# A two-layer decoder trunk on one core: queries and keys projected token-major, normed and then turned; scores of two query blocks together; inverse roots as a power on GpSimd

## The chip, the core and the metric

The kernel runs on one core of a Trainium2 chip. TensorE (PE) multiplies matrices into PSUM, VectorE (DVE), ScalarE (ACT) and GpSimd (POOL) work on SBUF tiles of 128 partitions, SyncE (SP) issues the loads. The metric is the device time of one execution in microseconds.

## What is computed

Two layers on x of 512 tokens by 1024 features, float32. Layer 0: RMS norm, one projection to 16 heads of 64 (8 forgetting heads and 8 stick-breaking heads, and 8 gate logits), causal attention, output projection, residual, then a gated MLP with a width-3 convolution. Layer 1: a gated short convolution in place of attention, and such an MLP. The change touches layer 0's attention and, in one helper, all four norms:

```python
xn = rms_norm(h, norm_g)
proj = xn @ w_in
q, k, v = heads(...), heads(...), heads(...)        # 16 heads of 64
q_fox, k_fox = rms_norm(q[:, :8], fox_q_g), rms_norm(k[:, :8], fox_k_g)
q_sb, k_sb = rms_norm(q[:, 8:], sb_q_g), rms_norm(k[:, 8:], sb_k_g)
# forgetting: softmax(q k / 8 + F_q - F_k) v;  F: running sum of log_sigmoid(gate)
# stick-breaking: sigmoid(z) times the product of sigmoid(-z) over later keys, times v
h = h + concat(o_fox, o_sb) @ w_out
```

## The kernel before

Activations stay on the chip with features on partitions: `hs_hi` and `hs_lo` are [128, 8, 512], feature block by token. Float32 products are three single-pass products of halves, x = hi + lo with hi rounded to float32r: hi hi, lo hi, hi lo. A weight chunk (512 KB) is loaded by SP (L220), its high half made by ACT (L223) and its low half by DVE (L226); three chunks are kept split, and `weights()` has `AHEAD` = 2 asked for in advance. The norm's scale by token is not applied to the input but to the products.

PSUM has eight banks under three names: two of `a` (projections, weighted sums, output), four of `b` (scores), two of `c` (transposes, small sums).

Queries and keys (`queries_keys`, L497) come by pairs of heads, p = 0 to 7, four forgetting pairs first. The weights stand in PE and 512 tokens stream by (L237 to L239, 24 products of 512 columns a bank), so the result has head features on partitions. ACT squares the bank (L552) and copies it out with the gain (L560, or L556 for a stick-breaking query). A norm over a head's 64 features is a sum over partitions: four matmuls of the squares with two columns of ones (L511, each a step of its own, `SUM_STEP` apart), then Newton's method for the inverse root in 12 DVE instructions (`rsqrt`, L299), a copy that spreads the result over 64 columns (L535), transposes to get it along the tokens (L542), a product (L544) and the split into halves (L320, L321). A stick-breaking query keeps its scale apart; the sigmoids take it as their scale (L600, L601).

Values (`values`, L459) are token-major: 128 tokens of `hs` stand in PE, 256 weight columns (four heads; 264 with the gates) stream by (L480 to L482), and ACT and DVE scale the bank by token on the way out (L473, L474).

`logits(p, b)` (L563) gives the scores of a pair's two heads for 128 queries: three products of 64 rows per head (L576), the decay (L580), the mask (L582), into two banks `b`; then softmax (L591 to L596) or the two sigmoids, a product scan and a product (L600 to L604). `turn` (L609) transposes the weights (L623) and splits them (L626, L627); `weigh` (L630) multiplies them by the values (L642, L643) and adds the two halves (L652, L653).

The program's order is written out by hand. `spend` counts PE microseconds emitted, `after` puts a step behind so many of them, `fill(us)` emits from `fillers`, a list of generators of independent products (projections of later pairs, values, the first half of the output projection). For block g the main loop (L750) emits the scores of block g, a fill of `FILL1`, every second time the weighted sum of block g - 2, the turning of block g - 1 and a fill of `FILL2`. `need` emits fillers until something is there. The framework's scheduler may move an instruction past others of its engine whose inputs it expects later. At the start, the first queries and keys run while x arrives and its norm is made; the norm's scale comes from `Norm.scale` (L267), its row form from `spread` (L274) after `NROWS`.

Of the kernel before, what the change touches and what calls it, by code (L numbers as in the profile page):

```python
# [20 lines left out]
I32 = mybir.dt.int32  # L21
# [17 lines left out]
WB = 4  # L39
PRE = 12.0  # L40
# [3 lines left out]
SUMS, ROWS = 3.0, 5.0  # L44
NSUMS, NROWS = 4.0, 3.0
FILL1, FILL2 = 1.0, 2.6
# [3 lines left out]
def trunk(  # L50
# [48 lines left out]
    # a row a column of `gains`: the norms after the first and the conv taps  # L99
# [27 lines left out]
    head_ones = const.tile([P, 2], F32, tag="head_ones", name="head_ones")  # L127
    pool.memset(head_ones, 0.0)
    pool.memset(head_ones[0:HD, 0:1], 1.0)
    pool.memset(head_ones[HD:P, 1:2], 1.0)  # L130
# [104 lines left out]
    def mm3(acc, w, rhs, first, last):  # L235
        """acc += w.T @ rhs of two pairs of halves."""
# [10 lines left out]
    class Norm:  # L247
        """Gathers the squares of a block's input and gives its RMS scale by token:
        `col` [token, block] on partitions and `row` along the free axis on all of them."""
# [17 lines left out]
        def scale(self, sums):  # L267
# [3 lines left out]
            rsqrt(self.col, v, NB, self.name)  # L271
# [11 lines left out]
        def scaled(self, fn):  # L283
            """Runs what needs `row` when it is there."""
# [14 lines left out]
    def rsqrt(dst, v, n, name):  # L299
        """dst = v ** -0.5 by Newton's method."""  # L300
        def t(tag, dt=F32):
            return tiny.tile([P, n], dt, tag=f"{tag}{n}", name=f"{tag}_{name}")
        half = t("rh")
        dve.tensor_scalar(half, v, -0.5, None, op0=ALU.mult)
        shifted = t("rs", I32)
        dve.tensor_scalar(shifted, v.bitcast(I32), 1, None, op0=ALU.logical_shift_right)
        guess = t("rg", I32)
        dve.tensor_scalar(guess, shifted, -1, 0x5F3759DF, op0=ALU.mult, op1=ALU.add)
        y = guess.bitcast(F32)
        for i in range(3):  # L310
            a = t("ra")
            dve.tensor_tensor(a, y, y, op=ALU.mult)
            b = t("rb")
            dve.tensor_tensor(b, a, half, op=ALU.mult)
            z = dst if i == 2 else t("ry")
            dve.scalar_tensor_tensor(z, b, 1.5, y, op0=ALU.add, op1=ALU.mult)
            y = z
# [5 lines left out]
    def causal_conv(dst, src, tap):  # L323
        """dst[t] = tap(2) src[t] + tap(1) src[t-1] + tap(0) src[t-2]."""
# [9 lines left out]
    def want_qk(p):  # L334
        want(w_in, 0, 8, D + p * P, P)
        want(w_in, 0, 8, p * P, P)

    def want_v(g):
        for k in range(0, 8, 4):
            want(w_in, k, 4, 2 * D + g * 256, 256, *((QKV, 8) if g == 0 else ()))  # L340
# [5 lines left out]
    want_qk(0)  # L346
    for g, ps_ in enumerate(((1, 2), (3, 4), (5, 6), (7,))):
        if g == 0:
            want_v(0)
        for p_ in ps_:  # L350
            want_qk(p_)
        if g < 3:
            want_v(g + 1)
# [39 lines left out]
    # ================= attention =================  # L393
# [4 lines left out]
    def choose():  # L398
        """Columns of 0 and 1 that pick the rows of `dl` and `dr`."""
# [25 lines left out]
    def log_gate():  # L425
        """The gates' log-sigmoid, its running sums on the partitions of `dl`."""
# [6 lines left out]
        wide = work.tile([P, S], F32, tag="u0", name="fwide").rearrange("p (b c) -> p b c", b=NB)  # L433
# [6 lines left out]
    def decay(wide):  # L440
# [9 lines left out]
        both = work.tile([P, S], F32, tag="u0", name="fboth")  # L450
# [8 lines left out]
    def values(g):  # L459
# [37 lines left out]
    def queries_keys(p):  # L497
# [12 lines left out]
        def sums(i, sq, b, t):  # L510
            pe.matmul(t[:, 2 * b:2 * b + 2], sq[:, b * P:(b + 1) * P], head_ones, start=True, stop=True)  # L511
            if b == NB - 1:
# [4 lines left out]
                if i == 1:  # L517
                    scales()
# [386 lines left out]
```

## Time and profile before

| | |
|---|---|
| three runs | 1233.95, 1235.51, 1236.94 us; median 1235.51 |
| the profiled execution | span 1231.8 us from the first to the last instruction; its time outside the span is not recorded |
| instructions | 14998, of them 5861 matmuls |
| engines, share of the span | PE 99%, weight loads 80%, DVE 62%, ACT 41%, POOL 2% |
| mean granted TensorE clock | 0.997 |
| loads | 108.13 MB, 88 GB/s over the span |

The profile is one execution seen by the hardware's profiler. A row of instructions gives start, duration, engine, line, operation, operands, shape; two or more of a kind in a row are merged (x4). A matmul's record runs on until its last result is modelled to be out, so the records of a stream overlap, and its true pace is the distance between starts. A group's row gives count, busy time and the mean of one in nanoseconds, then the engine's idle time before them and what ended it.

### The profile page before, as it was taken

How to read it: one execution, taken by the hardware profiler on the slowest of the kernel's cores; microseconds unless marked ns; L12 is line 12 of the kernel's file. 1: busy time of each engine (PE TensorE's matmuls, PEld its weight loads, DVE VectorE, ACT ScalarE, POOL GpSimd, SP SyncE). 2: the span in 40 equal slices, each digit the busy share in tenths (PEclk: the TensorE clock that was granted, in tenths of full speed). 3: DMA queues.
4: the chain of work that ended last, by engine and by line, in shares of the span. 5: the costliest groups of instructions: out<-in, count | busy, mean ns of one | idle time of the engine just before them, and what ended most of it. 6: DMA issues, size and time to landing. Idle time of an engine off the chain costs nothing.

```text
span 1231.8 us, 14998 instructions
## 1 busy us (share of the span) xinstructions
PE 1214.5 (99%) x5861; PEld 987.9 (80%) x5861; DVE 762.9 (62%) x1256; ACT 500.7 (41%) x779; POOL 21.5 (2%) x104
## 2 busy tenths in 40 slices
PE   8999999999999999999999999999999999999998
PEld 7887878767888888888888888888888888888886
DVE  5786878887776777673333555555767776762222
ACT  6455665655443434342222222233444434342120
POOL 3000000000000000000000000000000000000000
PEclk9999999999999999999999999999999999999999
DMA  6312121212333332323333333332333333322330
GB/s 177 104 36 69 36 69 36 69 52 69 95 93 100 89 102 86 103 79 95 94 94 101 91 97 99 89 101 87 91 98 92 96 95 93 98 91 86 118 105 35
DMA packets 183463, 108.13 MB, mean 88 GB/s; under 512 B 4604, under 2 KB 176684, under 8 KB 183392
## 3 DMA queue, kind: packets, MB, share of 16 engines
q1 hardware_dynamic: 183136, 107.01, 29.5%
q8 instruction: 46, 0.75, 0.3%
q0 software_dynamic: 256, 0.16, 0.1%
q14 instruction: 25, 0.20, 0.0%
HBM read 105.06 MB, written 2.10 MB: 87 GB/s over the span
## 4 chain that ended last, share of the span: by engine, by line
PE 94%; DVE 4%; ACT 1%; DMA 1%; issue 0%; SPq 0%; DVEq 0%; ACTq 0%
PE psa L237 13%; PE psa L239 13%; PE psa L238 13%; PE psb L237 11%; PE psb L239 11%; PE psb L238 11%; PE psa L480 3%; PE psa L482 3%; PE psa L481 3%; PE psb L481 2%; PE psb L480 2%; PE psb L482 2%; PE psb L576 1%; DVE rest L603 1%; PE psc L623 1%; PE psa L642 1%
## 5 line engine op out<-in xcount | busy, mean ns | idle before, releaser
L223 ACT ACTIVATE whi<-raw 128x1024 fp32r<-128x1024 f32 (+1 forms) x198 | 208.3, 1053 | 365.9 <-PE psb L238 127.0
L226 DVE TENSOR_TENSOR wlo<-raw,whi 128x1024 fp32r<-128x1024 f32 (+1 forms) x198 | 240.1, 1213 | 162.3 <-ACT whi L223 161.4
L237 PE MATMUL psa<-hs_hi,whi 128*128 128x512 f32 x544 | 220.4, 405 | 0.5 <-DVE o L653 0.5
L239 PE MATMUL psa<-hs_hi,wlo 128*128 128x512 f32 x544 | 215.5, 396 | 0.0
L238 PE MATMUL psa<-hs_lo,whi 128*128 128x512 f32 x544 | 215.0, 395 | 0.0
L237 PE MATMUL psb<-hs_hi,whi 128*128 128x512 f32 x480 | 189.9, 396 | 0.0
L239 PE MATMUL psb<-hs_hi,wlo 128*128 128x512 f32 x480 | 189.8, 395 | 0.0
L238 PE MATMUL psb<-hs_lo,whi 128*128 128x512 f32 x480 | 188.8, 393 | 0.0
L328 DVE SCALAR_TENSOR_TENSOR u<-y,taps,u 128x510 f32<-128x510 f32 (+1 forms) x176 | 131.0, 747 | 3.0
L239 PEld LDWEIGHTS psa<-hs_hi,wlo 128*128 128x128 f32 x544 | 102.2, 188 | 24.0
L237 PEld LDWEIGHTS psa<-hs_hi,whi 128*128 128x128 f32 x544 | 102.7, 189 | 21.8 <-PE psb L582 0.6
L238 PEld LDWEIGHTS psa<-hs_lo,whi 128*128 128x128 f32 x544 | 102.6, 189 | 21.4
L238 PEld LDWEIGHTS psb<-hs_lo,whi 128*128 128x128 f32 x480 | 90.1, 188 | 21.4
L239 PEld LDWEIGHTS psb<-hs_hi,wlo 128*128 128x128 f32 x480 | 90.1, 188 | 21.4
L237 PEld LDWEIGHTS psb<-hs_hi,whi 128*128 128x128 f32 x480 | 90.3, 188 | 20.3
L779 DVE TENSOR_TENSOR y<-psb,nrow_n 128x512 f32<-128x512 f32 x44 | 30.4, 691 | 83.9 <-PE psb L239 83.9
L320 ACT ACTIVATE a<-u 128x512 fp32r<-128x512 f32 x44 | 27.8, 633 | 118.7 <-DVE u L784 118.7
L783 ACT ACTIVATE u<-u 128x512 f32<-128x512 f32 x44 | 27.8, 632 | 91.4 <-DVE u L328 91.4
L325 ACT ACTIVATE u<-y,taps 128x512 f32<-128x512 f32 x88 | 62.9, 717 | 0.0
L321 DVE TENSOR_TENSOR a<-u,a 128x512 fp32r<-128x512 f32 x44 | 30.4, 692 | 29.4 <-ACT a L320 29.4
L480 PE MATMUL psa<-whi,hs_hi 128*128 128x256 f32 (+1 forms) x128 | 38.6, 303 | 0.0
L482 PE MATMUL psa<-whi,hs_lo 128*128 128x256 f32 (+1 forms) x128 | 36.2, 283 | 0.0
(226 smaller groups left out, 1851.0 us busy)
## 6 DMA issues: line engine op xcount, KB each, us to landing
raw<-in_ffn_w_up SPq DMA_DIRECT2D x88, 512.0 KB, 3.8
raw<-in_ffn_w_down SPq DMA_DIRECT2D x30, 512.0 KB, 3.7
raw<-in_attn_w_in SPq DMA_DIRECT2D x24, 512.0 KB, 3.9
raw<-in_conv_w_in SPq DMA_DIRECT2D x24, 512.0 KB, 3.8
raw<-in_ffn_w_down SPq DMA_DIRECT2D x16, 448.0 KB, 3.7
raw<-in_attn_w_out SPq DMA_DIRECT2D x8, 512.0 KB, 3.4
raw<-in_conv_w_out SPq DMA_DIRECT2D x8, 512.0 KB, 3.9
x_tok<-in_x SPq DMA_DIRECT2D x4, 512.0 KB, 7.9
```

The lines of the kernel that those rows point to most:

```text
L223: made = act.activation(hi[:, 0:nk * n], raw[:, 0:nk * n], AF.Copy)
L226: dve.tensor_tensor(lo[:, 0:nk * n], raw[:, 0:nk * n], f32(hi[:, 0:nk * n]), op=ALU.subtract)
L237: pe.matmul(acc, w[0], rhs[0], start=first, stop=False)
L238: pe.matmul(acc, w[0], rhs[1], start=False, stop=False)
L239: pe.matmul(acc, w[1], rhs[0], start=False, stop=last)
L321: dve.tensor_tensor(lo, src, f32(hi), op=ALU.subtract)
L325: act.activation(dst, src, AF.Copy, scale=tap(2))
L328: dve.scalar_tensor_tensor(dst[:, d:], src[:, 0:S - d], tap(j), dst[:, d:], op0=ALU.mult, op1=ALU.add)
L480: pe.matmul(acc, lhs[0], w[0], start=first, stop=False)
L481: pe.matmul(acc, lhs[0], w[1], start=False, stop=False)
L482: pe.matmul(acc, lhs[1], w[0], start=False, stop=last)
L779: dve.tensor_tensor(y, acc, norm.row, op=ALU.mult)
```

## The change

Queries and keys are projected like the values, in four groups of four heads (`columns`, `heads`), values of group 0 first. Each block of 128 tokens is then normed where a head's features lie along the free axis: ACT squares, DVE sums by head, POOL makes the scale in three steps, DVE multiplies from PSUM. `turn_heads(p)` transposes the normed block of a pair and splits it with the gain on the way out; both kinds of heads have their scale in the queries. `rsqrt` becomes one POOL instruction with a power, in the four norms as well. `logits` and `turn` take two query blocks at a time: four banks `b` at once, one tile of weights per head. A filler can be held back until its tiles are free, and the quotas are others (`PRE`, `FILL2`, a `FILL1` in `turn` after each block and one ahead of it). The comments' removal is left out here, and so are the old `queries_keys`, printed above, and the old `rsqrt`.

```diff
-WB = 4
-PRE = 12.0
+PRE = 3.0
-FILL1, FILL2 = 1.0, 2.6
+FILL1, FILL2 = 1.0, 3.3
...
+    minus_half = const.tile([P, 4], F32, tag="minus_half", name="minus_half")
+    pool.memset(minus_half, -0.5)
...
+    held_back = {}
+    def free(gen):
+        return gen not in held_back or held_back[gen]()
     def fill(us):
         quota[0] += us
         while quota[0] > 0 and fillers:
+            if not free(fillers[0]):
+                quota[0] = 0
+                break
...
+    def rsqrt(dst, v):
+        pool.tensor_tensor(dst, v, minus_half[:, 0:v.shape[1]], op=ALU.pow)
...
+    def want_group(kind, g):
         for k in range(0, 8, 4):
+            want(w_in, k, 4, (D, 0, 2 * D)[kind] + g * 256, 256, *((QKV, 8) if (kind, g) == (2, 0) else ()))
...
+    for g in range(4):
+        for kind in (0, 1, 2) if g else (2, 0, 1):
+            want_group(kind, g)
...
+    def columns(g, width=256):
         ws = [weights(), weights(AHEAD - 1)]
         for b in range(NB):
             acc = bank("a")
             tok = slice(b * P, (b + 1) * P)
             for k in range(ND):
                 w = ws[k // 4]
+                mm3_rhs(acc[:, 0:width], (hs_hi[:, k, tok], hs_lo[:, k, tok]), (w[0][:, k % 4, :], w[1][:, k % 4, :]), k == 0, k == ND - 1)
+                spend(0.36)
+                yield b, acc, k == ND - 1
...
+    def heads(i, g):
+        kept = normed[i, g] = [work.tile([P, 2, 256], F32, tag=("u0", "u1")[i], name=f"qk{i}{g}{j}", bufs=2 + i) for j in range(2)]
+        for b, acc, last in columns(g):
+            yield 1
+            if not last:
+                continue
+            by_head = acc[:, 0:256].rearrange("p (h d) -> p h d", d=HD)
+            sq = work.tile([P, S], F32, tag="sq", name=f"sq_{i}{g}{b}")[:, 0:256]
+            act.activation(sq, acc[:, 0:256], AF.Square)
+            total, r = (tiny.tile([P, 4], F32, tag=n, name=f"{n}{i}{g}{b}") for n in ("qv", "qr"))
+            dve.tensor_reduce(total, sq.rearrange("p (h d) -> p h d", d=HD), axis=AX.X, op=ALU.add)
+            pool.tensor_scalar(r, total, rx2[:, b:b + 1], EPS, op0=ALU.mult, op1=ALU.add)
+            rsqrt(r, r)
+            pool.tensor_scalar(r, r, norm.col[:, b:b + 1], None, op0=ALU.mult)
+            dve.tensor_tensor(
+                kept[b // 2][:, b % 2, :].rearrange("p (h d) -> p h d", d=HD), by_head,
+                r[:, :, None].to_broadcast([P, 4, HD]), op=ALU.mult,
+            )
+        done.add(("normed", i, g))
+    def turn_heads(p):
+        halves[p] = {}
+        for i in range(2):
+            need(("normed", i, p // 2))
+            t = bank("c")
+            for b in range(NB):
+                src = normed[i, p // 2][b // 2][:, b % 2, (p % 2) * P:(p % 2 + 1) * P]
+                pe.transpose(t[:, b * P:(b + 1) * P], src, ident)
+            spend(0.45)
+            g = head_gains[:, (0 if p < 4 else 2) + (1 - i):][:, 0:1]
...
+            act.activation(hi, t, AF.Copy, scale=g)
+            dve.scalar_tensor_tensor(lo, t, g, f32(hi), op0=ALU.mult, op1=ALU.subtract)
+    def logits(p, half):
...
+        both = [(b, e) for b in (2 * half, 2 * half + 1) for e in range(2)]
+        ss = {be: bank("b") for be in both}
...
         for step, (ql, kl) in enumerate(((q_hi, k_hi), (q_hi, k_lo), (q_lo, k_hi))):
+            for be in both:
+                rows, tok, keys = of(*be)
+                pe.matmul(ss[be][:, keys], ql[rows, tok], kl[rows, keys], start=step == 0, stop=False)
...
+                act.activation(rest[:, 0:n], s[:, 0:n], AF.Sigmoid, scale=-1.0)
+                act.activation(w, s[:, 0:n], AF.Sigmoid)
...
+            spend(0.22 * (b + 1))
+            fill(FILL1)
...
-    qk0 = queries_keys(0)
+    v0 = values(0)
...
     for k in range(ND):
-        next(qk0)
+        next(v0)
...
-    run(qk0)
     load_small()
-    run(values(0))
+    run(v0)
+    run(heads(0, 0))
     log_gate()
     load_gains()
+    run(heads(1, 0))
+    for g in range(1, 4):
+        fillers.extend((heads(0, g), heads(1, g), values(g)))
+        held_back[fillers[-3]] = lambda g=g: 2 * g - 1 in halves
+        held_back[fillers[-1]] = lambda g=g: g < 2 or 2 * g - 3 in weighed
     waiting = {}
+    turn_heads(0)
+    turn_heads(1)
     fill(PRE)
+    for u in range(16 + 2):
+        p, half = divmod(u, 2)
+        if u < 16:
+            waiting[u] = logits(p, half)
+            if u % 4 == 3 and p < 7:
+                turn_heads(p + 1)
+                turn_heads(p + 2)
             fill(FILL1)
+        if u >= 2:
+            weigh(*divmod(u - 2, 2))
+            if u - 2 == 7:
                 fillers.append(output(0, residual))
+        if 1 <= u <= 16:
+            fill(FILL1)
+            turn(*divmod(u - 1, 2), waiting.pop(u - 1))
             fill(FILL2)
```

More of the change, by code (lines that the diff above doesn't have):

```diff
@@ L581, in logits @@
-        for e in range(2):
-            pe.matmul(ss[e][:, tok], ident16, masks[0 if fox else 1], start=False, stop=True)
-        spend((4 if fox else 3) * wide * 0.00044 + 0.12)
-        ws = []
-        for e in range(2):
-            s = ss[e]
-            w = aw.tile([P, S], F32, tag="w", name=f"w{p}{b}{e}", bufs=WB)
-            ws.append(w)
+            for be in both:
+                rows, tok, keys = of(*be)
+                pe.matmul(ss[be][:, keys], dl[rows, p, tok], dr[rows, keys], start=False, stop=False)
@@ new lines, in logits @@
+        for be in both:
+            pe.matmul(ss[be][:, of(*be)[1]], ident16, masks[0 if fox else 1], start=False, stop=True)
+        spend((4 if fox else 3) * (0.4, 0.23)[half == 0] + 0.5)
+        ws = {}
+        tiles = [aw.tile([P, (3, 7)[half], P], F32, tag=f"w{half}", name=f"w{p}{half}{e}", bufs=2) for e in range(2)]
+        for b, e in both:
+            s, n = ss[b, e], (b + 1) * P
+            w = tiles[e].rearrange("p k c -> p (k c)")[:, (b % 2) * (n - P):][:, 0:n]
+            ws[b, e] = w
@@ L654, in weigh @@
         split(o_hi[:, p % 4, to], o_lo[:, p % 4, to], total)
+        if half:
+            weighed.add(p)
     def output(g, done):
```

191 lines of the change are left out of this document (36 added, 155 removed).

## The prediction

> **What bounds the kernel now.** I read the page first, then the windows, then the order of single instructions on PE, and last the evacuations on ACT and DVE. The page's first part says PE is occupied almost all the time; the windows (columns: stretch, its length, then busy time and count of PE, weight loads, DVE, ACT, POOL, then granted clock, DMA share, GB/s) say where it is not.
>
> ```profile
> PE 1214.5 (99%) x5861; PEld 987.9 (80%) x5861; DVE 762.9 (62%) x1256; ACT 500.7 (41%) x779; POOL 21.5 (2%) x104
> 13.20:25.70 12.50, 12.50 (x55) 9.89 (x54) 9.20 (x26) 11.06 (x19) 3.70 (x7) 0.95 0.47 126
> 25.70:55.90 30.20, 30.20 (x201) 26.93 (x199) 21.88 (x57) 14.68 (x23) 0.53 (x1) 1.00 0.39 105
> 55.90:180.00 124.10, 122.96 (x853) 103.04 (x853) 96.99 (x274) 74.62 (x180) 6.67 (x32) 1.00 0.21 56
> 180.00:284.00 104.00, 97.31 (x606) 77.92 (x604) 86.41 (x193) 61.54 (x129) 4.92 (x28) 0.98 0.16 49
> ```
>
> Everything that the change touches lies before 284 us; behind it the MLPs and the convolution stay as they are, so what attention gains or loses moves the end by as much. Within attention PE is without idle time up to 55.9, idle 1.1 us in the forgetting heads (to 180) and 6.7 us in the stick-breaking heads (to 284). So PE's own work sets the pace, and time comes from instructions taken off PE, as long as no new wait opens. Busy time hides gaps below the length of a modelled matmul, so I cost PE work by the distance from one start to the next. The rows that carry the prices, PE in order of time (start, duration, line, operation, count):
>
> ```profile
> 50.48 0.40 PE L239 MATMUL psa<-hs_hi,wlo 128*128 128x512 f32 x1
> 50.72 0.28 PE L511 MATMUL psc<-head_ones,sq 128*128 128x2 f32 x2
> 50.86 0.48 PE L237 MATMUL psa<-hs_hi,whi 128*128 128x512 f32 x1
> 51.18 0.39 PE L238 MATMUL psa<-hs_lo,whi 128*128 128x512 f32 x1
> ...
> 53.94 0.39 PE L238 MATMUL psa<-hs_lo,whi 128*128 128x512 f32 x1
> ...
> 55.56 0.39 PE L239 MATMUL psa<-hs_hi,wlo 128*128 128x512 f32 x1
> 55.88 0.39 PE L576 MATMUL psb<-qk_hi,qk_hi 64*128 64x256 f32 x2
> 56.11 0.28 PE L576 MATMUL psb<-qk_lo,qk_hi 64*128 64x256 f32 x2
> 56.23 0.28 PE L576 MATMUL psb<-qk_hi,qk_lo 64*128 64x256 f32 x2
> 56.34 0.28 PE L580 MATMUL psb<-dr,dl 64*128 64x256 f32 x2
> 56.56 0.28 PE L582 MATMUL psb<-mask,ident 128*128 128x128 bf16 x2
> 56.65 0.48 PE L237 MATMUL psa<-hs_hi,whi 128*128 128x512 f32 x1
> 56.97 0.40 PE L238 MATMUL psa<-hs_lo,whi 128*128 128x512 f32 x1
> ...
> 147.63 0.28 PE L482 MATMUL psa<-whi,hs_lo 128*128 128x256 f32 x1
> 147.75 0.60 PE L542 MATMUL psc<-ident,qwide 128*128 128x128 f32 x4
> 148.10 0.37 PE L480 MATMUL psa<-whi,hs_hi 128*128 128x256 f32 x1
> 148.31 0.28 PE L481 MATMUL psa<-wlo,hs_hi 128*128 128x256 f32 x1
> ...
> 149.84 0.28 PE L482 MATMUL psa<-whi,hs_lo 128*128 128x256 f32 x1
> ```
>
> A 512-wide product costs (55.56 - 53.94) / 7 steps = 0.231 us; a 256-wide one, as `values` already uses, (149.84 - 148.31) / 13 = 0.118. Every interruption of such a stream costs more than its own instructions: the first product behind it takes 0.32 instead of 0.23 (50.86 to 51.18), or 0.21 instead of 0.12 (148.10 to 148.31).
>
> **The change on PE, part by part.**
>
> *Sums of squares by matmul go.* One step costs 51.18 - 50.48 less two plain products: 0.70 - 0.46 = 0.24. There are 8 pairs x 2 x 4 blocks = 64, at most 15.2 us; a few stand back to back, at least 64 x 0.14 = 9.0 (50.72 to 50.86). I take 14.0, since most stand alone. The norm's scale no longer is spread to rows by transposes: 148.31 - 147.63 less two products of 0.118 is 0.44 for a set of four, 12 sets, 5.3 us. Added are the turns of the normed queries and keys: 16 sets of four, 7.1 us alone, less where four sets stand together: 6.8.
>
> *Projections token-major.* 16 x 24 = 384 products of 0.231 (88.9 us) become 2 x 4 groups x 4 blocks x 24 = 768 of 0.118 (90.4): +1.5.
>
> *Scores of two query blocks together.* A group of scores costs 56.97 - 55.56 less two products, 0.95. The second block of a merged group adds only four pairs of 0.12 and two masks, some 0.12 (56.56 to 56.65 is 0.09): 0.60. So 0.35 is saved 16 times: 5.6 us.
>
> PE work: -14.0 - 5.3 + 6.8 + 1.5 - 5.6 = -16.6 us.
>
> **What it costs elsewhere.** *The start.* Values now come first, and their banks can't be emptied before the norm's scale is there; before, the first keys and queries (11.1 us of products) needed no scale to be emptied. PE, ACT, DVE and POOL around that time:
>
> ```profile
> 13.10 0.78 PE L237 MATMUL psa<-hs_hi,whi 128*128 128x512 f32 x1
> 14.10 0.75 PE L687 MATMUL psb<-ident,x_tok 128*128 128x128 f32 x4
> 22.90 0.20 ACT L702 ACTIVATION_READ_ACCUMULATOR sq<-x_tok 128x1 f32 x1
> 23.14 0.17 DVE L269 TENSOR_SCALAR nv_n<-sums 128x4 f32<-128x4 f32 x1 [0.72 <-ACT sq L702]
> 25.40 0.16 DVE L316 SCALAR_TENSOR_TENSOR ncol_n<-rb_n,ry_n 128x4 f32<-128x4 f32 x1
> 30.37 0.47 ACT L473 ACTIVATE v<-psa,ncol_n 128x256 fp32r<-128x256 f32 x1 [1.49 <-issue]
> 30.87 0.48 DVE L474 SCALAR_TENSOR_TENSOR v<-psa,ncol_n,v 128x256 fp32r<-128x256 f32 x1 [0.73 <-ACT v L473]
> 31.27 0.22 DVE L476 SCALAR_TENSOR_TENSOR gate<-psa,ncol_n,f_bias 128x8 f32<-128x8 f32 x1
> 5.20 0.20 POOL L411 TENSOR_TENSOR two<-one 128x8 f32<-128x8 f32 x1
> ```
>
> The power on POOL isn't in this trace. Its nearest row is POOL's small add (L411, 0.20 us); the other end is the DVE chain that it replaces, 25.56 - 23.31 = 2.2. I take 0.5, near the add, as one instruction of the same size with more arithmetic. The Trainium skill ("GPSIMD Engine Reference", section "Engine selection") speaks against the move: elementwise work belongs on VectorE, GpSimd being about twice as slow for two inputs. For operands this small no such factor shows here: L411's 0.20 stands beside 0.16 to 0.17 for DVE's rows.
>
> So the scale is there at 23.31 + 0.5 + two hand-overs of 0.04 (22.90 + 0.20 to 23.14), 23.9, and the first bank is free 0.47 + 0.48 + 0.22 later, about 25.2. PE begins at 13.1 and has only two banks `a` to fill: 2 x 24 x 0.12 = 5.8 us, and 0.8 of transposes. It idles 25.2 - 13.1 - 6.6 = 5.5 us. Such a gap also lowers the clock. Before shows it at its end (the second row waits; the window behind):
>
> ```profile
> 274.38 0.40 PE L239 MATMUL psa<-o_hi,wlo 128*128 128x512 f32 x1
> 277.00 0.92 PE L623 MATMUL psc<-ident,w 128*128 128x128 f32 x4 [2.21 <-DVE pt L627]
> 276.00:279.40 3.40, 2.19 (x10) 1.82 (x11) 3.34 (x7) 2.49 (x5) 0.00 (x0) 0.68 0.02 5
> ```
>
> After a hole of 2.4 us the clock was 0.68 for 3.4 us, about 1.1 us lost. Start: +6.6 (6.3 and 8.3 with the power's two ends). The Trainium skill ("TensorE: Matmul & The Clock Gate", Part 1) has the clock fall after at least one idle window of about 3.4 us; by that rule holes under 3.4 us would be free of it, where this row shows one that is not.
>
> *The chain that empties a bank.* Each block of queries or keys now keeps its bank until ACT has squared it, DVE summed it, POOL made three steps and DVE multiplied it. By the nearest rows of the same width:
>
> ```profile
> L626 ACT ACTIVATE pt<-psc 128x256 fp32r<-128x256 f32 x16 | 5.5, 394 | 4.5 <-PE psc L623 4.5
> L591 DVE TENSOR_REDUCE top<-psb 128x1 f32<-128x256 f32 x8 | 3.1, 419 | 2.0 <-PE psb L582 2.0
> L627 DVE TENSOR_TENSOR pt<-psc,pt 128x256 fp32r<-128x256 f32 x16 | 6.3, 416 | 1.1 <-ACT pt L626 0.9
> ```
>
> 0.16 (a product's record outlasts its 0.12 step) + 0.39 + 0.42 + (0.2 + 0.5 + 0.2) + 0.42 + six hand-overs of 0.04 is 2.5 us. DVE is busy 72% of 25.7 to 55.9 and 83% of 180 to 284, so I add 0.3 for each of three entries into ACT's and DVE's queues: 3.4. With two banks and 2.8 us of products a block, eight blocks in a row at the front take (2.8 + 3.4) / 2 each: 8 x 0.3 = +2.4 us. Later other PE work stands between blocks.
>
> *Joins.* Four times (after the first group, then where a new group is asked for) the turns stand right behind the last block that they need, and PE meets that chain. Fillers emitted behind can be ordered into the hole; I charge 0.5 each, +2.0, between 0 and 4 x 2.8.
>
> *The end.* The quotas come to 3 + 1 + 15 x 7.3 + 6.3 = 119.8 us, and `need` pulls some 14.5 ahead of them, for 3 x 96 x 0.36 + 32 x 0.65 = 124.5 us of fillers. They run out about 10 us early, so the last two units have no cover. The hole above then is longer, as two blocks' scans stand in it: +1.5 (0 to 4).
>
> *In between.* DVE loses the Newton steps, the wide copies and one product per pair, and gets a reduction and a product per block; the distance from scores to turning grows from one block to two. Of the 6.7 idle microseconds after 180 some 2 should go. Against it, weighing shares the two banks with blocks that hold them longer: +1. Together -1.0. The scale of the other three norms is used `NROWS` = 3 us of products later, which hides the power up to that length: 0, and at most 3 x 2.2 were it as slow as the chain that it replaces and no product left to stand before it. POOL's queue also issues the small loads (most of its 3.70 us between 13.2 and 25.7); ordered ahead of the first power they could hold it back by up to that, but DVE hands its input over only at 23.31, so 0.
>
> *Weights.* A projection now holds two of the three split chunks for four blocks. The next group's second chunk is split when block 3 has passed its first half, and is wanted 2.9 us later. By these rows that takes 1.05 + 1.21 us:
>
> ```profile
> L223 ACT ACTIVATE whi<-raw 128x1024 fp32r<-128x1024 f32 (+1 forms) x198 | 208.3, 1053 | 365.9 <-PE psb L238 127.0
> L226 DVE TENSOR_TENSOR wlo<-raw,whi 128x1024 fp32r<-128x1024 f32 (+1 forms) x198 | 240.1, 1213 | 162.3 <-ACT whi L223 161.4
> ```
>
> 0.6 is left for both queues: 0, and with 0.3 of waiting at each of 11 borders +3.
>
> Sum: -16.6 + 6.6 + 2.4 + 2.0 + 1.5 - 1.0 = -5.1. The profiled execution shows a span of 1231.8; the median of the runs is 1235.5, and the 3.7 us around the span stay. So 1230.4 us.
>
> **Rivals.** *More of it arrives* (the order hides joins and front chain, the stick-breaking waits vanish): -16.6 + 6.6 - 4 and little else, about -14, 1221.5. For it: PE idles only 1.1 us in 124 between 55.9 and 180, so the order has so far been filled well. Against: the added chains run over four engines.
>
> *The banks are let go too late, and it becomes slower.* Place: banks `a`, in all 32 blocks of queries and keys. A unit of two blocks' scores lasts some 13 us (228 us between 55.9 and 284 in 16 units, less the saving) and asks for 3.5 banks (7.3 us of fillers at 8 x 0.36 a block, and one weighing), so from a chain of about 3.5 us on, each further microsecond costs half of it in 24 blocks, and in the eight at the front as well: 16 us for each microsecond. The gain of 5.1 is gone at 3.8 us; at 4.4 it is +9.7, 1245. A power that in effect is something slower on POOL than one short instruction would end here too. For it: DVE at 83%, a power between 0.2 and 2.2. Against: most neighbours of its price are short, and values, which have the same two banks, run densely now.
>
> *The joins stay open, no change.* If only the 0.5 us that `need` emits itself covers each, 4 x 2.3 = 9.2 instead of 2.0: +2.1, 1237.6; with half of that, 1234. This also is where it ends if DVE, not PE, paces the stick-breaking heads, so that their half of the saved PE work buys nothing.
>
> **How the numbers follow.** 0.2% (2.5 us) is about what a measurement of this kernel can tell from no change. Forecast (1225 to 1233) 0.42, more of it 0.17, no change 0.17, slower 0.24; hence faster 0.59, same 0.17, slower 0.24. The first case's own range is 1225 to 1233; 1219 to 1243 leaves out the tip of the gain and the long chains, some 0.2.
>
> **What would show it.** Right: no sum-of-squares matmuls and half as many groups of scores on PE; 256-wide products at 0.118; a hole on PE around 20 to 25 us with a lowered clock behind it; the stretch up to the end of attention's weighing (284 here) some 5 us shorter. Wrong: a power row much beyond 0.5 us; PE rows of the query and key projections that wait for the multiplying DVE row between 56 and 230 us (second rival); turns that wait 2 us or more at the joins (third); a busy PE without holes from 13 to 26 us.

## The result, and the profile after

The changed kernel takes 1279.5 us (median of four runs, 1274.9 to 1280.7) beside 1235.6 for the kernel before: a ratio of 1.0355, 95% interval 1.0334 to 1.0376. It is 44 us slower, where 5 us faster was forecast and 1243 was the upper end of the range. The profiled execution took 1279.3 us with a span of 1277.5.

First the page's line of the engines.

```profile
PE 1225.3 (96%) x6133; PEld 1017.2 (80%) x6133; DVE 747.5 (59%) x1112; ACT 492.6 (39%) x783; POOL 85.1 (7%) x202
```

Then the windows of attention (columns as in the prediction; the last one ends just behind attention's last weighted sum, as 284 does in the kernel before).

```profile
13.00:26.00 13.00, 9.71 (x62) 8.79 (x60) 8.70 (x17) 10.50 (x20) 4.30 (x8) 0.88 0.50 136
26.00:60.00 34.00, 29.30 (x230) 28.58 (x229) 17.03 (x40) 10.94 (x19) 10.36 (x17) 0.95 0.28 79
60.00:120.00 60.00, 52.12 (x401) 47.53 (x402) 39.95 (x99) 28.84 (x71) 20.58 (x40) 0.91 0.19 53
120.00:180.00 60.00, 54.47 (x441) 50.54 (x439) 38.51 (x100) 29.91 (x76) 16.73 (x35) 0.97 0.14 39
180.00:240.00 60.00, 53.37 (x398) 48.52 (x398) 37.74 (x77) 30.39 (x74) 14.29 (x36) 0.91 0.17 50
240.00:328.40 88.40, 74.18 (x454) 63.26 (x454) 63.11 (x110) 43.20 (x97) 9.34 (x30) 0.88 0.16 48
```

The whole loss lies here: attention's last weighing ends at 327.9 instead of 282.3, 45.6 us later, and the span is 45.7 us longer. In these 315.4 us PE is busy 273.2, so idle 42.2; before it was idle 7.8 of 270.8 (12.5 + 30.2 + 124.1 + 104.0, less 262.97 busy). Idle time grew by some 34 us, and busy time by 10, although PE has less to do: the granted clock is low in every window. Its shortfall, one less the clock times the length, adds up to 26 us over these rows; in the prediction's rows of before it is 2.7. No engine became the bound: by the same rows DVE is busy 65% of the time, less than before (79%), and POOL 24%. What became long is a wait, and the waits of DVE and of PE name it (the line that waits, the line waited for: us in total, times, longest):

```profile
DVE qk L498 <- POOL qr L497: 46.2, 31, 1.9
PE psa L466 <- DVE qk L498: 16.8, 7, 6.0
PE psc L581 <- DVE pt L585: 5.8, 4, 2.9
PE psa L601 <- DVE qk L498: 3.0, 2, 2.2
...
PE psc L282 <- POOL ncol_n L304: 2.7, 1, 2.7
```

L498 is the multiplication that ends the norm of a block. DVE reaches it, finds POOL's scale unfinished, and stands still, 31 times of 32. POOL's three steps, as groups (count, busy time, mean of one in ns):

```profile
L304 POOL TENSOR_TENSOR qr<-qr,minus_half 128x4 f32<-128x4 f32 x32 | 36.1, 1129 | 2.7
L495 POOL TENSOR_SCALAR qr<-qv,rx 128x4 f32<-128x4 f32 x32 | 14.5, 453 | 122.2 <-DVE qv L494 122.2
L497 POOL TENSOR_SCALAR qr<-qr,ncol_n 128x4 f32<-128x4 f32 x32 | 9.9, 308 | 3.1
```

The power takes 1.13 us in the mean (1.04 in the median), not 0.5, and the three steps 1.89 in the mean, not 0.9. One block of this chain in an ordinary stretch, on ACT, DVE and POOL:

```profile
101.17 0.39 ACT L492 ACTIVATE sq<-psa 128x256 f32<-128x256 f32 x1 [2.37 <-PE psa L468]
101.58 0.42 DVE L494 TENSOR_REDUCE qv<-sq 128x4 f32<-128x256 f32 x1 [0.31 <-ACT sq L492]
102.10 0.27 POOL L495 TENSOR_SCALAR qr<-qv,rx 128x4 f32<-128x4 f32 x1 [2.81 <-DVE qv L494]
102.45 1.04 POOL L304 TENSOR_TENSOR qr<-qr,minus_half 128x4 f32<-128x4 f32 x1
103.59 0.30 POOL L497 TENSOR_SCALAR qr<-qr,ncol_n 128x4 f32<-128x4 f32 x1
103.92 0.42 DVE L498 TENSOR_TENSOR qk<-psa,qr 128x256 f32<-128x256 f32 x1 [1.92 <-POOL qr L497]
104.33 1.62 DVE L550 TENSOR_REDUCE top<-psb 128x1 f32<-128x384 f32 x3
```

From 101.17 to 104.34 are 3.2 us, about the 3.4 of the prediction. It is the shortest form: from the start of the square to the end of the multiplication 13 of the 32 blocks take 3.1 to 3.2 us, the median is 3.7, the mean 4.3, and the last two blocks, at the join shown below, take 6.6 and 9.0. Even in the short form DVE idles 1.92 us between its two instructions, and the score reductions (L550) stand in its queue behind the multiplication: they begin the moment it ends, without a wait of their own. The longest hole on PE is a join, from 244.5 to 250.6; PE, then DVE and POOL:

```profile
243.70 0.82 PE L512 MATMUL psc<-ident,qk 128*128 128x128 f32 x6
250.55 0.55 PE L466 MATMUL psa<-whi,hs_hi 128*128 128x256 f32 x1 [6.03 <-DVE qk L498]
...
243.33 2.33 DVE L561 TENSOR_TENSOR_SCAN rest<-rest 128x511 f32<-128x511 f32 x2
245.57 1.26 DVE L562 TENSOR_TENSOR w<-w,rest 128x511 f32<-128x511 f32 x2
246.75 0.41 DVE L494 TENSOR_REDUCE qv<-sq 128x4 f32<-128x256 f32 x1
247.08 1.22 DVE L230 TENSOR_TENSOR wlo<-raw,whi 128x1024 fp32r<-128x1024 f32 x1
249.98 0.42 DVE L498 TENSOR_TENSOR qk<-psa,qr 128x256 f32<-128x256 f32 x1 [1.68 <-POOL qr L497]
...
247.26 1.17 POOL L495 TENSOR_SCALAR qr<-qv,rx 128x4 f32<-128x4 f32 x1 [8.02 <-DVE qv L494]
```

The sum by head (L494) stands behind the scans of the stick-breaking blocks, and POOL's first step lasts 1.17 us instead of 0.27, beside DVE's L230. PE stands still meanwhile, and the windows around the hole show what follows it:

```profile
244.60:248.00 3.40, 0.00 (x0) 0.00 (x0) 3.40 (x5) 2.29 (x4) 0.74 (x1) 1.00 0.00 0
248.00:251.40 3.40, 0.85 (x5) 0.89 (x5) 1.72 (x4) 0.00 (x0) 2.34 (x4) 0.52 0.49 154
251.40:254.80 3.40, 3.40 (x18) 3.38 (x17) 1.54 (x3) 0.25 (x1) 1.93 (x3) 0.50 0.50 151
```

The clock is 0.50 in the last of these windows, in which PE is busy throughout, so the hole of 6.0 us costs about 1.7 more behind it. The other three joins have the same kind of hole: 3.3 us at 61, 1.8 and 1.4 at 112 and 115, 2.2 and 1.5 at 177 and 182. With the 6.0 that is 16 us at four joins.

### The profile page after: what moved, and what is told of

Its sections match the earlier page's. It is cut to its first block, busy times and chain, and to the rows that moved or that the text cites. A ratio compares the mean times of both kernels' runs of the same rounds, so it can differ in the third digit from the quotient of the medians.

```text
span 1277.5 us, 15525 instructions
## 1 busy us (share of the span) xinstructions
PE 1225.3 (96%) x6133; PEld 1017.2 (80%) x6133; DVE 747.5 (59%) x1112; ACT 492.6 (39%) x783; POOL 85.1 (7%) x202
## 4 chain that ended last, share of the span: by engine, by line
PE 86%; DVE 6%; POOL 3%; ACT 2%; issue 1%; DMA 1%; SPq 0%; DVEq 0%; ACTq 0%
PE psb L241 11%; PE psb L243 11%; PE psa L241 11%; PE psb L242 11%; PE psa L243 11%; PE psa L242 11%; PE psa L466 4%; PE psa L468 4%; PE psa L467 4%; POOL qr L304 2%; PE psb L467 2%; PE psb L466 2%; PE psb L468 2%; DVE rest L561 1%; PE psc L581 1%
## 5 line engine op out<-in xcount | busy, mean ns | idle before, releaser
L227 ACT ACTIVATE whi<-raw 128x1024 fp32r<-128x1024 f32 (+2 forms) x198 | 208.3, 1052 | 363.0 <-PE psb L242 131.2
L230 DVE TENSOR_TENSOR wlo<-raw,whi 128x1024 fp32r<-128x1024 f32 (+2 forms) x198 | 240.3, 1213 | 161.4 <-ACT whi L227 160.4
L241 PE MATMUL psa<-hs_hi,whi 128*128 128x512 f32 x416 | 164.7, 396 | 0.0
L243 PE MATMUL psa<-hs_hi,wlo 128*128 128x512 f32 x416 | 164.2, 395 | 0.0
L466 PE MATMUL psa<-whi,hs_hi 128*128 128x256 f32 (+1 forms) x384 | 117.8, 308 | 22.8 <-DVE qk L498 16.8
L467 PE MATMUL psa<-wlo,hs_hi 128*128 128x256 f32 (+1 forms) x384 | 112.5, 293 | 0.1
L468 PE MATMUL psa<-whi,hs_lo 128*128 128x256 f32 (+1 forms) x384 | 112.6, 293 | 0.0
L466 PEld LDWEIGHTS psa<-whi,hs_hi 128*128 128x128 f32 x384 | 77.1, 201 | 27.6 <-issue 19.4
L467 PEld LDWEIGHTS psa<-wlo,hs_hi 128*128 128x128 f32 x384 | 77.4, 202 | 0.3 <-DVE wlo L230 0.3
L468 PEld LDWEIGHTS psa<-whi,hs_lo 128*128 128x128 f32 x384 | 77.3, 201 | 0.0
```

The costliest lines, as they stand in the source:

```text
L227: made = act.activation(hi[:, 0:nk * n], raw[:, 0:nk * n], AF.Copy)
L230: dve.tensor_tensor(lo[:, 0:nk * n], raw[:, 0:nk * n], f32(hi[:, 0:nk * n]), op=ALU.subtract)
L241: pe.matmul(acc, w[0], rhs[0], start=first, stop=False)
L243: pe.matmul(acc, w[1], rhs[0], start=False, stop=last)
L466: pe.matmul(acc, lhs[0], w[0], start=first, stop=False)
L467: pe.matmul(acc, lhs[0], w[1], start=False, stop=False)
```

## The experiments

The theory after this reading: the chain over POOL holds DVE's queue, leaves the joins open, and the holes lower the clock. The first rival is the prediction's second one: the chain holds PE's two banks too long. The second is that another part of the change, the merged scores, costs the time. All runs are medians of four or more; differences below 3 us are not read. Behind each time stand in brackets the ratio to the kernel before, run beside it, and its 95% interval.

**The banks.** ACT copies the bank out at once, and DVE multiplies the copy in place (first kernel); in the second POOL multiplies it, the last change of the diff.

```diff
             act.activation(sq, acc[:, 0:256], AF.Square)
+            flat = kept[b // 2][:, b % 2, :]
+            act.activation(flat, acc[:, 0:256], AF.Copy)
+            by_head = flat.rearrange("p (h d) -> p h d", d=HD)
...
-            dve.tensor_tensor(
+            pool.tensor_tensor(
```

> The changed kernel, but ACT copies each projected block out of its bank at once (behind the square), into the tile in which DVE then multiplies it in place. The bank is free after two ACT steps; DVE still waits for POOL's scale in its queue. Changed kernel: 1279.5 us, and PE's waits for the multiplying DVE row (L498) some 25 us there. Theory 'banks' (PE waits because the chain holds the two banks): the waits go and with them the lowered clock, 1240 to 1250. Theory 'DVE's queue' (the multiply stands at the head of DVE's queue until POOL is done, 46 us of idle DVE, and everything behind it is late): 1268 to 1280. Theory 'scores' (two query blocks at once bunch the work of ACT and DVE): 1270 to 1280.

> As the copy-out kernel, and POOL does the multiply as well, so that no DVE instruction of the projections waits for POOL. Theory 'banks': no better than the copy-out kernel, within 5 us of it. Theory 'DVE's queue': the 46 us of DVE idling go, 1230 to 1245, at least 15 us below the copy-out kernel. Theory 'scores': above 1260.

Measured: 1275.7 (1.0324, 1.0307 to 1.0342) and 1263.7 (1.0231, 1.0208 to 1.0254). Free banks give 3.8 us where 30 to 40 were expected of them: the place where the prediction's slower rival puts the loss is not where most of it arises. The waits of the first, then of the second kernel:

```profile
DVE qk L501 <- POOL qr L500: 44.7, 28, 2.1
PE psc L515 <- DVE qk L501: 14.0, 7, 3.8
```

```profile
PE psc L515 <- POOL qk L501: 17.6, 7, 5.9
```

With the banks free, PE waits at the turns (L515) instead. With the multiplication on POOL DVE no longer waits, and 12 us come back, less than the 15 or more that the theory of DVE's queue had asked for; the turns still wait.

**The power's price.** In the 32 blocks alone, the power becomes a multiplication (their scale is then another number than the reference's).

```diff
-            rsqrt(r, r)
+            pool.tensor_tensor(r, r, minus_half, op=ALU.mult)
```

> The power in the 32 projected blocks is a multiplication on POOL instead (the scale of queries and keys is then not the reference's); the norms keep their power. The power takes 1.04 us, a small POOL operation 0.2 to 0.3, so each chain is 0.75 us shorter. Both 'banks' and 'DVE's queue': each of 32 chains gives back up to 0.75 us, and some holes fall under the length that lowers the clock, 1250 to 1265. Theory 'scores': 1274 to 1280. If it comes to 1240 or less, the price of the power alone is the cause.

Measured: 1262.4 (1.0214, 1.0186 to 1.0242), 17 us less than the changed kernel. POOL's step and DVE's wait there:

```profile
L496 POOL TENSOR_TENSOR qr<-qr,minus_half 128x4 f32<-128x4 f32 x32 | 8.6, 268 | 2.7
```

```profile
DVE qk L498 <- POOL qr L497: 22.9, 27, 1.1
```

The step falls from 1129 to 268 ns, 27.5 us over 32 blocks, and DVE's wait from 46.2 to 22.9. In the other direction, the power in the kernel before in place of its Newton steps, one instruction of 16 columns for each pair of heads and one of four columns for each of the four norms:

```diff
     def rsqrt(dst, v, n, name):
-        def t(tag, dt=F32):
...
+        pool.tensor_tensor(dst, v, minus_half[:, 0:n], op=ALU.pow)
```

> The kernel before with its Newton steps replaced by the power on GpSimd, for the pairs of heads (16 columns) and the four norms; nothing else. Its scale chain goes over POOL in the middle of DVE's queue, but only 8 times, and ACT empties the banks without it. Theory 'DVE's queue': each of 8 chains holds DVE for some 2 us that it spent on Newton steps before, so within 6 us of 1235. Theory 'the power itself is the cause': 1245 or more.

Measured: 1250.8 (1.0124, 1.0109 to 1.0139): 15.5 us slower by this part alone, pairs and norms together. POOL's group and DVE's wait in that kernel:

```profile
L302 POOL TENSOR_TENSOR qr<-qv,minus_half 128x16 f32<-128x16 f32 x8 | 23.3, 2916 | 63.9 <-DVE qv L509 63.9
```

```profile
DVE qr L512 <- POOL qr L302: 22.7, 8, 3.0
```

Sixteen columns take 2.92 us, four 1.01 to 1.04 in the medians, and DVE stands behind all of it, 22.7 us, where its own twelve short steps kept it at work.

**The merged scores.** Three runs: the changed kernel with the old `logits`, `turn` and loop, one block at a time (`FILL2` 2.65, `WB` 4); the kernel before with the new ones (`FILL2` 3.2, fewer buffers for the Newton steps); and the changed kernel without the per-head norm, so that only token-major projection, turns and merged scores are left (queries and keys go on with the token's scale alone).

```diff
-            act.activation(sq, acc[:, 0:256], AF.Square)
...
-                r[:, :, None].to_broadcast([P, 4, HD]), op=ALU.mult,
-            )
+            act.activation(kept[b // 2][:, b % 2, :], acc[:, 0:256], AF.Copy, scale=norm.col[:, b:b + 1])
```

> The changed kernel's projections, norms and turns of queries and keys, with scores and turned weights one query block at a time as before (FILL1 1.0, FILL2 2.65, so that as much is filled per unit). Theory 'scores': most of the loss goes, 1235 to 1250. Theories 'banks' and 'DVE's queue': it stays or gets worse, since the same chains now meet twice as many groups, 1275 to 1295.

> The kernel before with scores and turned weights of two query blocks together (four banks at once, FILL1 ahead of and in the turning, FILL2 3.2), its projections and Newton steps as they were. By the prediction's term the merging alone saves 5.6 us of PE work: 1228 to 1234. Theory 'scores' (the merged groups bunch ACT and DVE and PE waits for them): 1240 to 1255, and with the run that undid the merging (14.8 us better than the changed kernel) some 15 us above 1235 are expected.

> The changed kernel without the norm over a head's features: ACT copies each projected block out with the token's scale, and no square, sum, power or multiply of it is made (queries and keys are left un-normed). What is left is token-major projection, turning and merged scores. If the chain in all its forms is the cause, 1220 to 1232, the prediction's sum without its chain; what is above that is due to the start (5 to 7 us), the merged scores and the order of the fillers. Theory 'scores': still 1240 to 1255.

Measured: 1264.7 (1.0237, 1.0218 to 1.0256), 15 us less than the changed kernel; 1247.1 (1.0094, 1.0073 to 1.0115), 12 us more than the kernel before; 1237.2 (1.0018, 1.0007 to 1.0028), 42 us less than the changed kernel and still no gain. The second came out as the theory of the scores had it; the first and the third fell between the ranges of the theories, so merging is one part of the loss and the norm's chain another. Merging costs by itself. One place in the kernel before with merged scores, DVE and then PE:

```profile
278.35 1.22 DVE L606 TENSOR_TENSOR_SCAN rest<-rest 128x511 f32<-128x511 f32 x1
279.67 0.69 DVE L607 TENSOR_TENSOR w<-w,rest 128x511 f32<-128x511 f32 x1
280.28 1.22 DVE L606 TENSOR_TENSOR_SCAN rest<-rest 128x511 f32<-128x511 f32 x1
281.41 0.39 DVE L657 TENSOR_TENSOR o<-psa,o 64x256 f32<-64x256 f32 x1
...
282.43 0.43 DVE L657 TENSOR_TENSOR o<-psa,o 64x256 f32<-64x256 f32 x1
...
283.00 0.77 PE L237 MATMUL psa<-o_hi,whi 128*128 128x512 f32 x1 [3.24 <-DVE o L657]
```

A merged unit puts four scans (two query blocks of two heads) into DVE's queue at once, and the short step that empties a bank (L657) stands behind them; PE waits 3.24 us for it. Over this kernel PE waits 8.5 us for that step, over the kernel before 1.3 (L653 there). That merging costs is shown by the runs; that these bursts are the reason is read from such rows, and no run parted them from the changed places of the fills. The windows of that kernel behind 180:

```profile
180.00:240.00 60.00, 55.75 (x350) 47.53 (x349) 41.93 (x104) 31.25 (x67) 2.12 (x12) 0.95 0.17 54
240.00:297.00 57.00, 48.67 (x268) 38.65 (x268) 43.46 (x87) 30.24 (x61) 2.83 (x16) 0.91 0.15 47
```

PE is idle 12.6 us of these 117, before 6.7 of 104, and the clock fell with it.

**The joins.** The second kernel above (POOL multiplies), with 4 us of other work emitted between the last needed block and the turns at the three later joins.

```diff
+                for i in range(2):
+                    need(("normed", i, (p + 1) // 2))
+                fill_now(4.0)
                 turn_heads(p + 1)
```

> As the kernel in which POOL multiplies (1263.7 us), but at the three later joins 4 us of fillers are emitted between the last block that the turns need and the turns. Theory 'joins' (the turns stand right behind their last block, PE waited 17.6 us for POOL's multiply in 7 places): some 10 us and part of the lowered clock come back, 1246 to 1255. If the waits only move to other places, 1260 to 1266.

Measured: 1250.9 (1.0127, 1.0112 to 1.0142), 12.8 us less than without the cover. PE's wait for POOL at the turns falls from 17.6 to 7.0 us; its wait at the turned weights grows from 5.4 to 9.5.

**DVE's queue alone.** A first try issued the multiplication 3.4 us of matmuls later, and a second ran this with the old scores.

```diff
+            def multiply(b=b, by_head=by_head, r=r):
+                dve.tensor_tensor(by_head, by_head, r[:, :, None].to_broadcast([P, 4, HD]), op=ALU.mult)
...
+            if g:
+                after(3.4, multiply)
```

> As the changed kernel, with each bank copied out by ScalarE and the multiplication kept on VectorE, in place, but issued 3.4 us of matmuls later (in all groups but the first), so that VectorE's queue no longer stands behind the power; the turns ask for the later point, so fillers are issued until then. The theory that the queue behind the waiting multiplication and the open joins are what costs: the row of VectorE waiting for GpSimd falls from 46.2 us to under 12 (the first group's eight blocks), and the time to 1246 to 1255, about that of the kernel with the multiplication on GpSimd and covered joins (1250.9). The rival, that GpSimd's multiplication helped there because it took some 11 us of work from VectorE: 1258 or more.

> The same with the scores and turns of before, one block at a time. If the merged scores cost by themselves (11.8 us in the kernel before, 14.9 in the changed one), the two gains add: 1233 to 1241, about the time of the kernel before. If both remove the same waits, the second gives little: 1245 or more.

Measured: 1272.6 (1.0304, 1.0287 to 1.0321) and 1261.7 (1.0218, 1.0202 to 1.0233). The edit did not do what it was made for: DVE's wait was still 43.7 us, 29 times, so it says nothing about the queue. That the old scores gave 10.9 us here too is all that the pair shows. An ordering did it: with the bank copied out as before, the multiplication of a block stands behind the sum of the next one.

```diff
-            dve.tensor_reduce(total, sq.rearrange("p (h d) -> p h d", d=HD), axis=AX.X, op=ALU.add)
+            reduced = dve.tensor_reduce(total, sq.rearrange("p (h d) -> p h d", d=HD), axis=AX.X, op=ALU.add)
...
+            for earlier in held_mul:
+                behind(earlier(), reduced)
+            held_mul[:] = [lambda by_head=by_head, r=r: dve.tensor_tensor(
+                by_head, by_head, r[:, :, None].to_broadcast([P, 4, HD]), op=ALU.mult)]
```

> As the changed kernel with each bank copied out by ScalarE, and the multiplication of a block on VectorE ordered behind the sums of the next block, so that a whole block of TensorE's work lies between a block's power and the instruction that waits for it; only the last block of each group is multiplied at once. The joins are not covered. The theory that VectorE's queue behind the waiting multiplication is one of the costs (some 12 us of the 40 to 44): VectorE's row waiting for GpSimd falls from 44.7 us (with the bank copied out) to under 14, and the time from 1275.7 to 1260 to 1267, about that of the kernel with the multiplication on GpSimd (1263.7). The rival, that the gain there came from taking the multiplication off VectorE: 1271 or more though the row has fallen.

Measured: 1260.8 (1.0202, 1.0173 to 1.0232), 15 us less than with the copy alone; DVE's wait (under 14 was expected):

```profile
DVE qk L504 <- POOL qr L501: 15.3, 11, 1.9
```

DVE does the same work as in the first experiment, so the 15 us are the queue behind the waiting instruction; that POOL took work from DVE is not needed to explain its 12.

**All together, and without the norm.** The changed kernel without the per-head norm and with the old scores; then two forms with the norm, the old scores and covered joins, one with the ordered multiplication, one with POOL's.

> The changed kernel without the per-head norm (queries and keys go on with the token's scale alone) and with the scores and turns of before, one block at a time. If the token-major projection saves the some 8 us of TensorE work that the profile of the kernel without the norm shows, and the merged scores cost some 12 by themselves: 1222 to 1230, faster than the kernel before. If merging costs only behind a blocked VectorE: 1234 to 1239, the time of the kernel without the norm (1237.2).

> The same with the joins covered by 4 us of further work (it was worth 12.8 us) and with the scores and turns of before (10.9 to 14.9 us in four settings). If the three costs are separate: 1234 to 1242, no faster than the kernel before, since the norm's chain still holds up the start and some joins. If they are one cost seen three times: 1248 or more.

> The changed kernel with the bank copied out by ScalarE, the multiplication on GpSimd, the joins covered by 4 us of further work and the scores and turns of before: from the kernel with all of these but the last (1250.9), with the 10.9 to 14.9 us that the merged scores cost elsewhere: 1236 to 1240, no faster than the kernel before (1235.2), since the start's wait for the first power and the chain at the joins stay. If this form's scores do not wait for the merged blocks: 1246 or more.

Measured: 1225.1 (0.9920, 0.9906 to 0.9935), 1243.6 (1.0064, 1.0047 to 1.0081) and 1241.2 (1.0039, 1.0027 to 1.0052). The first is 10 us faster than the kernel before: the token-major projection is worth its PE work when nothing waits for a norm. The other two come 1 to 2 us above the ranges that adding the parts gave: the three costs are largely separate. Windows of the first, the sums of PE, weight loads, DVE, ACT and POOL last:

```profile
13.00:26.00 13.00, 9.27 (x61) 8.16 (x59) 8.65 (x19) 10.42 (x19) 3.75 (x7) 0.89 0.44 124
26.00:60.00 34.00, 34.00 (x279) 33.81 (x280) 16.33 (x32) 14.30 (x23) 0.00 (x0) 0.96 0.30 87
...
sum 261.20, PE 252.32 PEld 228.22 DVE 184.87 ACT 154.72 POOL 14.87; mean PE 42.05 PEld 38.04 DVE 30.81 ACT 25.79 POOL 2.48
```

Two last tries at a form with the norm that beats the kernel before: 8 us of cover at the joins, and 3.3 us of fillers a block in place of 2.65.

> As the last kernel (multiplication on GpSimd, joins covered, scores of before), with 8 us of further work in place of 4 between a join's last block and its turns. If the turns still wait for the chain at the joins (6.1 us in its row of TensorE waiting for GpSimd), that row goes and the time falls to 1234 to 1238. If what is left lies elsewhere (the wait for the weights' turns, 5.5 us, the start): 1239 to 1243.

> As that kernel with 4 us at the joins, but with 3.3 us of projections behind every block of turns in place of 2.65, so that projections run further ahead all along. If the blocks of scores wait for their chains because too little lies between them: 1234 to 1238. If the fillers then run out before the last pairs: 1243 or more.

Measured: 1242.2 (1.0060, 1.0044 to 1.0077) and 1245.7 (1.0091, 1.0076 to 1.0106). Neither helps: each fell in the second range given for it, not in the one for a gain. What PE waits for in the kernel with POOL's multiplication, 4 us of cover and old scores:

```profile
PE psc L520 <- POOL qk L506: 6.1, 3, 3.3
PE psc L586 <- DVE pt L590: 5.5, 2, 4.7
```

The kernel without the norm has of the second kind:

```profile
PE psc L568 <- DVE pt L572: 2.0, 2, 1.1
```

With 8 us of cover the first row still has 5.0, its longest 3.3 as well. The order of time says where they stand; PE in the kernel with 4 us of cover:

```profile
59.89 0.33 PE L520 MATMUL psc<-ident,qk 128*128 128x128 f32 x1 [1.66 <-POOL qk L506]
63.53 0.47 PE L520 MATMUL psc<-ident,qk 128*128 128x128 f32 x1 [3.31 <-POOL qk L506]
284.28 1.12 PE L586 MATMUL psc<-ident,w 128*128 128x128 f32 x4 [4.67 <-DVE pt L590]
```

The first two are the turns behind the first group, the one join that no run covered; with 8 us at the later joins the same waits of 1.66 and 3.31 are there, and nothing else is left in that row. The third is at the last turns of attention. No form tried with the norm's chain is faster than the kernel before.

## Why the prediction was wrong

**Right: PE's own work.** Without the merged scores the terms come to -14.0 - 5.3 + 6.8 + 1.5 = -11.0 us. In the kernel without norm and merging, whose PE instructions are these, PE is busy 252.3 us up to the end of weighing, beside 263.0 before: -10.7, with about the same shortfall of the clock (0.11 x 13 + 0.04 x 34 = 2.8, and 2.7). Pricing by the distance between starts held.

**Roughly right, mis-sized: the start and the chain.** PE waits 2.7 us for the first scale (L282 <- POOL L304 above), with a lowered clock behind it. 5.5 us of hole were forecast, and 3.7 is PE's idle time from 13 to 26 in the kernel without the norm. The chain that empties a bank, 3.4, is 3.2 in its shortest form but 4.3 in the mean of the 32 blocks. By the second rival's own price, 16 us for each microsecond beyond 3.8, the mean would cost 8 to 9 us; freeing the bank early was worth 3.8. So that rival's sign was right, and its place held only a small part of the loss.

**Failed: "The power on POOL ... I take 0.5".** It is 1.13 in the mean, 1.04 in the median. The argument, one instruction of the same size as an add, does not hold: with the same operands the multiplication takes 0.27 in the mean (0.20 in the median), and the power four to five times that. The whole of this difference, more than the step from 0.5 alone, was worth 17 us here; the power in place of Newton's steps cost 15.5 in the kernel before. The bounds, 0.2 to 2.2, held the size; the error was to let them enter the sum only through the chain's length.

**Failed: a wait without its queue.** The chain was costed as a latency that holds PE's bank, with 0.3 us for each entry into a queue. That DVE stands at L498 for as long as POOL works, with score reductions, splits and evacuations behind it, has no term: 46.2 us of DVE's time, 15 us of the kernel's by the ordered multiplication. The prediction named DVE's load (72 to 83%) but not who waits behind a waiting instruction.

**Failed: "Joins ... I charge 0.5 each".** In the changed kernel PE stands 16 us at the four joins, above even the 11.2 (4 x 2.8) taken as the upper end, so the third rival's joins did stay open. Covering the three later ones was worth 12.8 us, 4.3 each, in the form in which POOL also multiplies. DVE's queue delays the chain there, as at 246.75, and the clock falls behind the hole.

**Failed: merged scores, -5.6.** Merging costs 12 us alone; in the changed kernel and its variants taking it out gave 14.9, 12.1, 10.9 and 9.7. The saving on PE is there: in the kernel without the norm a merged group of a forgetting pair takes 1.52 us beside two plain products (from 62.80 to 64.56), and without merging a single group 0.93 (from 61.30 to 62.47), so 0.34 are saved where 0.35 was priced. The saved interruptions of PE were counted; that four blocks' scans and reductions enter DVE's queue together, ahead of the short steps for which PE waits, was not. "Some 2 us should go" from the stick-breaking heads' idle time went the other way.

**Failed: the clock.** One window after one hole was counted, 1.1 us. Over attention the shortfall is 26 us, spread over all windows, part of it while PE stands still; so holes cost more than their length, and each of the failed terms above makes them.

The 44 us then are: -10.2 for projection and turns with the start, +12.1 for merging (the two kernels without the norm), and +42.3 for the norm's chain with its work on ACT, DVE and POOL. Of the 42.3 the copied bank gives back 3.8, the queue (or POOL's multiplication) 12 to 15, the joins 12.8. Some 11 to 14 us are left; between the best form with the norm and the kernel without norm and merging lie some 15 to 16 (16.1 by the times, 14.7 by the ratios to the kernel before), so the parts overlap a little. The two waits above come to 11.6 us, beside 2.0 without the norm, before any loss of clock: 5.0 of them at the first join, which was never covered, and 4.7 at the last turns. What covering those would give, and which step of the chain holds the remainder, was not taken apart. Nor did any run keep the inverse root on DVE in the new layout, so what the move to POOL as such costs, beside the length of its instruction, stays open.

## What to carry to other kernels

Moving a short computation to an idle engine does not by itself shorten a chain: price the new instruction by its own kind, and ask of the engine that waits for it what stands behind it in its queue. If a result has to come back, put the next block's independent work in front of the instruction that needs it, by an ordering and not by a later place in the program. Joining blocks saves overhead on the engine that issues them and makes bursts on the engine that empties the banks; that engine's short steps should not stand behind them.

## What was not expected of the hardware

A power of 128x4 takes 1.04 us on POOL in the median of 32 (mean 1.13, longest 2.02), of 128x16 2.92, beside 0.20 (mean 0.27) for a multiplication of 128x4 with two tensors. POOL's first step of the chain took 0.27 us in one place and 1.17 where DVE ran its 1.22 us subtraction with two inputs in SBUF (247.08 and 247.26 above): both end within 0.13 us. In the changed kernel eight steps of the chain begin 0.1 to 0.3 us behind the start of such a subtraction (L230): five first steps, 1.17 or 1.18 us each, and three powers, 1.88 to 2.02, so all are 0.8 to 1.0 longer than usual. The Trainium skill ("SBUF — State Buffer", section "SBUF: two separate sides") says that such a DVE instruction and one of GpSimd hold a shared pair of ports in turn, for a whole instruction; these eight agree, and no run separated it from other causes. Where POOL's instruction began first, the power at 68.17 beside a subtraction at 68.25, both kept their usual 1.04 and 1.23 us, which is not what the rule says. The clock was 0.50 for a full 3.4 us window behind the hole of 6.0 us, and 0.55 behind the one at the start, which lasted 2.7:

```profile
25.90:29.30 3.40, 2.99 (x14) 2.90 (x14) 1.02 (x5) 0.58 (x2) 0.00 (x0) 0.55 0.00 0
```
